# Sums of yb on chip, x added in the output stage, and second products accumulated onto a bank that ScalarE filled

## The chip, the cores and the metric

The kernel runs on one core of a Trainium2 chip. TensorE (PE) multiplies into PSUM banks, VectorE (DVE), ScalarE (ACT) and GpSimd (POOL) work on elements, and SyncE (SP) mostly issues DMA transfers. POOL issues those that add to their destination; ACT can issue transfers too. The metric is the device time of one execution in microseconds (us); less is better.

## The reference

One decoder layer in float32 on 512 tokens of 1024 features. All matrix products of this text come from it:

```python
h = x @ w_in[i]
ua, va, za, qh, kh, vh, zb, ga, gb = jnp.split(h, IN_OFFSETS, axis=-1)
...
ya = ua * sa.reshape(bn, s_len, A_WIDTH) * jax.nn.silu(za)
...
yb = o.reshape(bn, s_len, B_WIDTH) * jax.nn.silu(zb)

merged = jax.nn.sigmoid(ga) * (ya @ w_branch_a[i]) + jax.nn.sigmoid(gb) * (yb @ w_branch_b[i])
mix_out = merged @ w_out[i]

ple = jax.nn.sigmoid(x @ w_ple_gate[i]) * (p[i] @ w_ple[i])

x = layer_norm(DEEPNORM_ALPHA * x + mix_out + ple, ln_g[i], ln_b[i])
```

`sa` is a gated product within chunks of the normalised gelu of `va`; `o` is differential attention with eight heads, RMS-normalised.

## The kernel before

**Precision.** Each operand is cut into a high part (rounded, type fp32r) and a low part (what is left); a product of two operands is three matmuls, high by high, high by low and low by high. ScalarE writes the high part of a weight (line 407) and VectorE the low part (line 410); 128x1024 elements at a time are one unit of 512 KB. `cut_part` does the same for an activation (ScalarE's high, then VectorE's low four matmuls later, line 1276).

**Quads.** Eight products of 512x1024 by 1024x1024 (named v, va, zq, ga, gb, pg, wb, wa) are made by Strassen's scheme in Winograd's form (seven products of quarters in place of eight). `quad` runs seven steps. A step is two halves (t = 0 and 1) of 12 matmuls, each half into a PSUM bank of its own, so a quad is 168 matmuls. Three pairs of banks are used: Y by steps 1 and 5 to 7, X by step 2, Z by steps 3 and 4. Step 1 makes the first product P1 in Y, step 2 makes P2 in X, and the sum P1 + P2 is the first quarter of the result. Before: ScalarE copies Y to SBUF behind step 1 (`keep`, line 658), and behind step 2 VectorE adds X to it (`block`, line 663). Y goes on accumulating from step 5.

The left operands of steps 1 and 2 and of the last are quarters themselves; those of steps 3 to 6 are sums and differences of quarters, called s1, n4, s2 and s3. For the quads on x they lie in two tiles `xsh` and `xsl` (high and low, four slots each); the same tiles, called `ys`, later hold the sums of yb, then those of ya.

**Weights.** The right operands are sums of quarters of the weight, too. Some are made ahead in DRAM. The others are made in place in a ring of eight buffers: once a unit has been cut, `follow` has POOL issue a DMA that adds the next quarter to the same buffer (line 382), so a chain of up to four units goes through one buffer, each link used two steps after the one before. wa has no sums made ahead and eight such transfers; gb and pg have six.

**Order.** Every engine takes its instructions in program order. The program is written along the matmuls: `later(n, fn)` runs `fn` when n more matmuls have been written. So a number in the tables at the head (YB11, GATES, RESIDUE, ...) says behind which matmul of its quad an operation stands in its engine's queue; it starts when it is at the head of that queue and its operands are there.

**Stages.** Attention with its projections, then ua and part of za, then the quads va, zq, ga, gb, pg, the small product ple (48 matmuls), the quads wb (yb) and wa (ya), and the output product: a first half of 96 matmuls, a second of 120. What the change touches:

- the sums of yb (`sums_of`): eight pieces. VectorE adds (line 728), ScalarE cuts (line 735), VectorE takes the low part (line 739), and ScalarE issues two stores of 256 KB a piece to DRAM (line 731), four pieces in the stage of ua and four in gb. In pg SP issues eight loads of 512 KB back into `ys` (line 1136).
- the sums of ya: POOL adds in place (line 1288) in pg and wb, then `cut_part`.
- `residue` (line 1330): for each of four row blocks POOL issues a DMA that adds 512 KB of x to `base`, from wb's 180th matmul on and 36 apart, which is in wa. `base` holds the embedding term; `residual` (line 1408) adds the output product to it.
- `mb_done` (line 1352) multiplies wb's blocks by their gate on VectorE. `merge` (lines 1385 and 1387) multiplies wa's blocks by their gate, adds wb's (POOL for the upper half of the tokens), and a number of matmuls later (`MERGE`) PE transposes the result (line 1393) through two banks, from which ScalarE (line 1396) and VectorE (line 1397) make the operands of the output product.

Of the kernel before, what the change touches and what calls it, by code (L numbers as in the profile page):

```python
# [70 lines left out]
SUMS_OF_Y = (84, 139, 162, 180, 43, 82, 113, 157)  # L71
# [4 lines left out]

HELD = 2
# [3 lines left out]
YA22, YA_S1, YA_S3, YA_CUT_S1 = (4, 35), (24, 60), (40, 76), (90, 97)  # L81
YB11, YB12, YB22, LOAD_YS = (28, 43), (52, 59), (170, 177), (76, 100, 124, 148)
# [5 lines left out]
MERGE = (24, 15)  # L88
RESIDUE = (180, 36)
# [154 lines left out]
def hybrid_layer(ctx: ExitStack, tc: tile.TileContext, a, out: bass.AP):  # L244
# [397 lines left out]
    def operands(h, l, parts, last=4):  # L642

        s1, s2, n4, s3 = parts if callable(parts[0]) else [of_sum(parts, c) for c in range(4)]
        return (of_parts(h, l, 0, 0), of_parts(h, l, 4, 0), s1, n4, s2, s3, of_parts(h, l, last, 2 * P))

    def quad(name, left, banks, place, done):
# [8 lines left out]
        def keep(key, bank):  # L656
            kept[key] = tmp[0](key[0])[:, :bank.shape[-1]]
            act.activation(kept[key], bank, AF.Copy)  # L658
# [33 lines left out]
        steps = ((Y, True, after1), (X, True, after2), (Z, True, after5), (Z, False, None),  # L692
# [19 lines left out]

    ysd = dram.tile([2, 8, P, T], F32, name="ysd")

    def sums_of(source, store_to, tile_of, kp, at, steps):
        made = {}

        def quarter(k, t):
            return source[:, k:k + 2, t * 2 * P:(t + 1) * 2 * P]

        def piece(j):
            x11, x12 = quarter(2 * kp, 0), quarter(4 + 2 * kp, 0)
            x21, x22 = quarter(2 * kp, 1), quarter(4 + 2 * kp, 1)
            op, x, y = ((OP.subtract, x21, x22), (OP.subtract, made.get(0), x11),
                        (OP.add, made.get(1), x12), (OP.subtract, x11, x21))[j]
            m, h, l = tile_of(j)
            made[j] = m
            dve.tensor_tensor(out=m, in0=x, in1=y, op=op)

            def store(i, part):  # L730
                act.dma_start(out=store_to[i, 2 * j + kp],
                              in_=part.rearrange("p a b -> p (a b)").bitcast(F32))

            def high():
                act.activation(h, m, AF.Copy)
                store(0, h)

            def low():
                dve.tensor_tensor(out=l, in0=m, in1=h.bitcast(F32), op=OP.subtract)
                later(5, store, 1, l)  # L740

            later(steps[0], high)
            later(steps[1], low)

        for i, n in enumerate(at):
            later(n, piece, i)
# [300 lines left out]
    y_made = []  # L1047

    def of_stacks(j):
        hl = ap_.tile([P, 2, 2, 2 * P], F32R, name="yhl", tag="k", bufs=3)  # L1050
        if j % 2 == 0:
            y_made.append(ap_.tile([P, 2, 2, 2 * P], F32, name="ym", tag="q", bufs=3))
        return y_made[-1][:, j % 2], hl[:, 0], hl[:, 1]

    sums_of(yb[0], ysd, of_stacks, 0, SUMS_OF_Y[:4], (10, 18))


# [75 lines left out]

    def load_sum(parts, source, c):
        for i, part in enumerate(parts):
            sp.dma_start(out=part[:, c].rearrange("p (e a) t -> p e (a t)", e=2).bitcast(F32),
                         in_=source[i, 2 * c:2 * c + 2].rearrange("e p t -> p e t"))
# [106 lines left out]
    y_tiles = []  # L1244

    def of_norm(j):
        if not y_tiles:
            y_tiles.extend(late.tile([P, 2, 2, 2 * P], F32 if n == "g" else F32R, name="ys" + n, tag=n) for n in "gb")
        return y_tiles[0][:, j % 2], y_tiles[1][:, 0], y_tiles[1][:, 1]

    sums_of(yb[0], ysd, of_norm, 1, SUMS_OF_Y[4:], (10, 18))
    quad("gb", of_x, pairs(True), lambda c, t: None, gate_done("gb"))
    phl = []

    def load_p():
        phl.append(late.tile([P, 2, 2, T], F32R, name="phl", tag="R"))
        for k in range(2):
            pt = tmp[0]("pt")
            sp.dma_start(out=pt, in_=a["pT"][k * P:(k + 1) * P, :])
            later(40 + 12 * k, cut, phl[0][:, 0, k, :], phl[0][:, 1, k, :], pt)  # L1260

    later(64, load_p)
    base = post.tile([P, NT, D], F32, name="base", tag="V")

    def embedding_gate(c, t, z, source):
        act.activation(z, source, AF.Sigmoid)
# [19 lines left out]
    def add_ya(to, op, x, y, part):  # L1286
        (z,), (x,), (y,) = (part_of((ua,), *q, part) for q in (to, x, y))
        pool.tensor_tensor(out=z, in0=x, in1=y, op=op)  # L1288

    def slot(c):  # L1290
        return lambda part: (tile[:, c, 2 * part:2 * part + 2, :] for tile in ys)
# [15 lines left out]
    in_parts(cut_ya, YA22, 1, 1, (0, 1))  # L1307
# [6 lines left out]
    for n, c in zip(LOAD_YS, (0, 2, 1, 3)):  # L1314
        later(n, load_sum, ys, ysd, c)
# [35 lines left out]
    def mb_done(c, t, z, source):  # L1351
        dve.tensor_tensor(out=z, in0=source, in1=gate.pop(("gb", c, t)), op=OP.mult)
# [18 lines left out]
    for t in range(NT):  # L1371
        later(RESIDUE[0] + RESIDUE[1] * t, residue, t)
    quad("wb", operands(xh, xl, ys), pairs(True), place_b, mb_done)
# [10 lines left out]
    def merge(c, t, z, source):  # L1384
        dve.tensor_tensor(out=z, in0=source, in1=gate.pop(("ga", c, t)), op=OP.mult)
        early = t < NT // 2
        (pool if early else dve).tensor_tensor(out=z, in0=z, in1=mb[0][:, t, c * T:(c + 1) * T], op=OP.add)
        later(MERGE[not early], merge_turn, c, t, z)

# [11 lines left out]
    quad("wa", operands(xh, xl, of_ya, 0), pairs(False), lambda c, t: None, merge)  # L1401
# [20 lines left out]

    units = []
# [80 lines left out]
```

## Time and profile before

| what | value |
|---|---|
| median of 3 runs | 630.97 us (630.57 to 633.01) |
| the profiled execution | 631.1 us, span 629.1 us |
| PE busy | 610.4 us, 97% of the span |
| DVE, ACT, POOL busy | 474.4, 337.9, 139.7 us |
| moved by DMA | 146.91 MB, 234 GB/s over the span |

The span goes from the first to the last instruction of the program; the execution's own time is longer. A matmul's end is modelled and matmuls overlap, so how fast PE runs is read from the starts of matmuls or from how many fall into a window. Names such as `wr<-in_w` are tiles: what is written, then what is read; `wh` and `wl` are a weight's high and low part, `xsh` and `xsl` the slots of sums, `ps_...` PSUM banks. A wait is put down to what ended last before it.

### The profile page before, as it was taken

To read this page: it belongs to the slowest core of one execution; us is meant where nothing else is said; L and a number is where in the kernel's file an instruction comes from. 1 tells how busy PE (TensorE), PEld (TensorE's weight loads), DVE (VectorE), ACT (ScalarE), POOL (GpSimd) and SP (SyncE) were. 2 spreads that over 40 slices of the span, in tenths; PEclk is the share of its full clock that TensorE was granted. 3 is DMA by queue.
4 is the path that set the end of the run, shared out by engine and by line. 5 is a ranking of instruction groups with operands and counts; after the bars stand their busy time and mean duration, and the time that the engine had idled before them with its cause. 6 is when DMAs were issued, how large, how long until landed. Compare 5 with 4: busy or idle time off the path is not lost.

```text
span 629.1 us, 8655 instructions
## 1 busy us (share of the span) xinstructions
PE 610.4 (97%) x3012; PEld 511.4 (81%) x3012; DVE 474.4 (75%) x800; ACT 337.9 (54%) x540; POOL 139.7 (22%) x144
## 2 busy tenths in 40 slices
PE   9999999999999999999999999999999999977995
PEld 6888888888888888888899888888778778766884
DVE  6996687788788767768578877678967796749376
ACT  6555654744745755489565655556653563424100
POOL 1234030341440530230111211113400322520012
PEclk9999999999999999999999999999999999988999
DMA  8689899587888796888988898899798489994002
GB/s 302 215 245 186 268 282 289 210 219 248 287 235 274 217 319 207 230 222 320 258 284 237 210 244 241 238 260 299 190 328 333 160 224 237 262 259 167 1 33 101
DMA packets 50111, 146.91 MB, mean 234 GB/s; under 512 B 6420, under 2 KB 7572, under 8 KB 49748
## 3 DMA queue, kind: packets, MB, share of 16 engines
q1 hardware_dynamic: 37268, 106.91, 47.9%
q0 software_dynamic: 9920, 34.87, 30.1%
q10 hardware_dynamic: 2880, 4.59, 2.0%
q8 instruction: 24, 0.39, 0.3%
q14 instruction: 19, 0.16, 0.1%
HBM read 123.14 MB, written 34.73 MB: 251 GB/s over the span
## 4 chain that ended last, share of the span: by engine, by line
PE 82%; DMA 7%; issue 5%; DVE 3%; ACT 1%; POOL 1%; DVEq 0%; POOLq 0%; ACTq 0%
PE ps_pp L278 51%; PE ps_sc L278 12%; DMA wr<-in_w 7%; PE ps_tx L278 7%; PE ps_sc L826 3%; PE ps_po L871 3%; PE ps_tr L860 1%; PE ps_po L278 1%; PE ps_tr L278 1%; DVE wl L410 1%; DVE xl L1276 1%; ACT wh L407 1%; POOL ua L1288 1%; PE ps_po L482 1%; PE ps_tr L1213 1%
## 5 line engine op out<-in xcount | busy, mean ns | idle before, releaser
L410 DVE TENSOR_TENSOR wl<-wr,wh 128x1024 fp32r<-128x1024 f32 (+1 forms) x143 | 178.7, 1254 | 46.9 <-ACT wh L407 46.4
L407 ACT ACTIVATE wh<-wr 128x1024 fp32r<-128x1024 f32 (+1 forms) x143 | 147.0, 1033 | 86.3 <-PE ps_sc L278 28.0
L278 PE MATMUL ps_pp<-xh,wh 128*128 128x512 f32 (+1 forms) x276 | 109.5, 397 | 0.0
L278 PE MATMUL ps_pp<-xl,wh 128*128 128x512 f32 (+1 forms) x276 | 107.0, 388 | 0.0
L278 PE MATMUL ps_pp<-xh,wl 128*128 128x512 f32 (+1 forms) x276 | 105.4, 382 | 0.0
L278 PE MATMUL ps_pp<-wl,xh 128*128 128x512 f32 (+1 forms) x168 | 64.6, 385 | 0.0
L278 PE MATMUL ps_pp<-wh,xh 128*128 128x512 f32 (+1 forms) x168 | 64.5, 384 | 0.0
L278 PE MATMUL ps_pp<-wh,xl 128*128 128x512 f32 (+1 forms) x168 | 64.5, 384 | 0.0
L839 ACT ACTIVATE p<-p,sth 128x128 f32<-128x128 f32 (+3 forms) x64 | 35.5, 555 | 47.4 <-DVE sth L837 47.3
L278 PEld LDWEIGHTS ps_pp<-xh,wl 128*128 128x128 f32 x276 | 52.1, 189 | 8.7
L278 PEld LDWEIGHTS ps_pp<-xh,wh 128*128 128x128 f32 x276 | 52.1, 189 | 8.6 <-ACT wh L304 0.7
L278 PEld LDWEIGHTS ps_pp<-xl,wh 128*128 128x128 f32 x276 | 52.1, 189 | 8.2 <-DVE xl L305 0.4
L382 POOL DMA_DIRECT2D wr<-in_w x34 | 29.8, 875 | 126.4 <-DVE wl L410 113.8
L771 POOL TENSOR_TENSOR hl<-m,hl 128x512 fp32r<-128x512 f32 x16 | 25.1, 1608 | 54.7 <-ACT hl L766 54.7
L278 PEld LDWEIGHTS ps_pp<-wl,xh 128*128 128x128 f32 x168 | 32.0, 190 | 6.2 <-DVE wl L410 0.3
L278 PEld LDWEIGHTS ps_pp<-wh,xl 128*128 128x128 f32 x168 | 32.0, 191 | 6.0
L278 PEld LDWEIGHTS ps_pp<-wh,xh 128*128 128x128 f32 x168 | 31.9, 190 | 6.1
L278 PE MATMUL ps_pp<-wh,xsh 128*128 128x512 f32 x80 | 32.2, 402 | 4.6 <-ACT s L658 4.6
L278 PE MATMUL ps_sc<-wl,xsh 128*128 128x512 f32 x88 | 34.5, 392 | 1.2 <-DVE wl L410 1.1
L833 DVE CUSTOM_DVE_ANT_0 p<-ps_sc,mask 128x128 f32<-128x128 f32 (+3 forms) x64 | 30.9, 483 | 5.6 <-PE ps_sc L826 5.6
L278 PE MATMUL ps_sc<-wh,xsh 128*128 128x512 f32 x88 | 34.5, 392 | 0.2 <-ACT s L658 0.2
L278 PE MATMUL ps_sc<-wh,xsl 128*128 128x512 f32 x88 | 34.3, 390 | 0.0
(312 smaller groups left out, 1267.3 us busy)
## 6 DMA issues: line engine op xcount, KB each, us to landing
wr<-in_w SPq DMA_DIRECT2D x81, 512.0 KB, 5.1
wr<-in_w POOLq DMA_DIRECT2D x30, 512.0 KB, 6.9
k<-hl SPq DMA_DIRECT2D x16, 256.0 KB, 5.4
q<-hl SPq DMA_DIRECT2D x16, 256.0 KB, 4.2
ws_va<-in_w POOLq DMA_DIRECT2D x8, 512.0 KB, 10.5
wr<-ws_va SPq DMA_DIRECT2D x8, 512.0 KB, 4.2
wa<-in_w POOLq DMA_DIRECT2D x6, 512.0 KB, 7.4
kx<-hl SPq DMA_DIRECT2D x12, 256.0 KB, 5.4
```

The costliest lines, as they stand in the source:

```text
L278: pe.matmul(ps, s, m, start=start, stop=stop, skip_group_check=read_within)
L382: pool.dma_start(out=raw[u][:, :n], in_=weights(STEPS[FOLLOWS[u]][1], n), accum_op=OP.add)
L407: act.activation(h, raw[u][:, :width(STEPS[u][0])], AF.Copy)
L410: dve.tensor_tensor(out=l, in0=raw[u][:, :width(STEPS[u][0])], in1=h.bitcast(F32), op=OP.subtract)
L482: pe.matmul(idle, zeros[:, :P], zeros, start=True, stop=True)
L771: pool.tensor_tensor(out=hl[:, 3 - j, :], in0=m[2 * j], in1=hl[:, j, :].bitcast(F32), op=OP.subtract)
L826: pe.matmul(sc[m][:, :n], q[:, m, i * P:(i + 1) * P], kk[:, m, :n], start=o == 0, stop=o == 1)
L833: dve.tensor_tensor_reduce(out=pr[m][:, :n], in0=sc[m][:, :n], in1=mask[:, T - n:], scale=-(DK ** -0.5), scalar=3e38, op0=OP.add, op1=OP.m ...
L839: act.activation(pr[m][:, :n], pr[m][:, :n], AF.Exp, bias=st[:, m:m + 1], scale=-1.0, accum_out=st[:, 2 + m:3 + m])
L860: pe.transpose(tr[:, j * P:(j + 1) * P], ad[:, j * P:(j + 1) * P], ident)
L871: pe.matmul(po[:, i * P:(i + 1) * P], at[:, j * P:(j + 1) * P], v[:, j, h * P:(h + 1) * P], start=j == 0, stop=j == i)
L1213: pe.matmul(sa[:, t * P:(t + 1) * P], va[:, t, g * P:(g + 1) * P], aux[0][:, 0, g, :], start=True, stop=True)
```

## The change

Three edits, with the numbers of the tables set anew.

1. The sums of yb are no longer made in `sums_of`, stored and loaded. POOL makes them in place in yb (`add_yb`, four adds in gb, four in pg), and `cut_part` cuts them straight into the slots of `ys` in pg, each behind the step that last reads the slot. The quarter 22 of yb is cut in gb into the quarter 21 of `xh` and `xl`, that of ya in ple into the quarter 22; wb and wa read them there. The sums of ya move from pg and wb to ple and wb.
2. In v, gb, pg, wb and wa (`GOES_ON`) ScalarE copies P1 from bank Y into bank X, and step 2 accumulates P2 onto it. VectorE's add of the first quarter falls away. What follows it (a sigmoid, a multiplication by the gate, in v a copy) reads bank X.
3. The four transfers of x are issued in the first half of the output stage, behind matmuls 2, 8, 26 and 32.

Beside these, POOL takes four multiplications from VectorE (two in `mb_done`, two in `merge`), and the later transposes of the merges stand 22 or 23 matmuls behind their merge, not 15.

```diff
+GOES_ON = ('v', 'gb', 'pg', 'wb', 'wa')
...
-MERGE = (24, 15)
-RESIDUE = (180, 36)
+MERGE = {'early': 24, 1: 23, 0: 22}
+RESIDUE = (2, 8, 26, 32)
...
+        goes_on = name in GOES_ON
+
         def after1(t):
-            keep(("s1", t), Y[t])
+            if goes_on:
+                act.activation(X[t], Y[t], AF.Copy)
+            else:
+                keep(("s1", t), Y[t])
 
         def after2(t):
+            if goes_on:
+                z = place(0, t)
+                return done(0, t, tmp[0]("s1")[:, :X[t].shape[-1]] if z is None else z, X[t])
             s1 = kept.pop(("s1", t))
             block(0, t, X[t], s1, OP.add, s1)
...
-        steps = ((Y, True, after1), (X, True, after2), (Z, True, after5), (Z, False, None),
+        steps = ((Y, True, after1), (X, not goes_on, after2), (Z, True, after5), (Z, False, None),
...
-    sums_of(yb[0], ysd, of_stacks, 0, SUMS_OF_Y[:4], (10, 18))
...
-    sums_of(yb[0], ysd, of_norm, 1, SUMS_OF_Y[4:], (10, 18))
...
+    def add(tile, to, op, x, y, part):
+        (z,), (x,), (y,) = (part_of((tile,), *q, part) for q in (to, x, y))
+        pool.tensor_tensor(out=z, in0=x, in1=y, op=op)
...
+    in_parts(cut_yb, YB22, 1, 1, (0, 1))
+    in_parts(add_yb, YB_S1, (1, 1), OP.subtract, (0, 1), (1, 1))
+    in_parts(add_yb, YB_S3, (0, 1), OP.subtract, (0, 0), (0, 1))
     quad("gb", of_x, pairs(True), lambda c, t: None, gate_done("gb"))
...
     in_parts(cut_yb, YB11, 0, 0, (0, 0))
     in_parts(cut_yb, YB12, 1, 0, (1, 0))
-    in_parts(cut_yb, YB22, 1, 1, (1, 1))
+    in_parts(add_yb, YB_S2, (0, 0), OP.subtract, (1, 1), (0, 0))
+    in_parts(add_yb, YB_N4, (1, 0), OP.add, (0, 0), (1, 0))
+    in_parts(cut_yb, YB_CUT_S1, 1, 1, slot(0))
+    in_parts(cut_yb, YB_CUT_N4, 1, 0, slot(2))
+    in_parts(cut_yb, YB_CUT_S2, 0, 0, slot(1))
+    in_parts(cut_yb, YB_CUT_S3, 0, 1, slot(3))
+    in_parts(cut_ya, YA22, 1, 1, (1, 1))
     in_parts(add_ya, YA_S1, (1, 1), OP.subtract, (0, 1), (1, 1))
     in_parts(add_ya, YA_S3, (0, 1), OP.subtract, (0, 0), (0, 1))
     in_parts(cut_ya, YA_CUT_S1, 1, 1, first_sum)
-    for n, c in zip(LOAD_YS, (0, 2, 1, 3)):
-        later(n, load_sum, ys, ysd, c)
...
     def mb_done(c, t, z, source):
-        dve.tensor_tensor(out=z, in0=source, in1=gate.pop(("gb", c, t)), op=OP.mult)
+        by = pool if c == 1 and t < 2 else dve
+        by.tensor_tensor(out=z, in0=source, in1=gate.pop(("gb", c, t)), op=OP.mult)
...
-    for t in range(NT):
-        later(RESIDUE[0] + RESIDUE[1] * t, residue, t)
...
     def merge(c, t, z, source):
-        dve.tensor_tensor(out=z, in0=source, in1=gate.pop(("ga", c, t)), op=OP.mult)
         early = t < NT // 2
+        by = pool if early and c else dve
+        by.tensor_tensor(out=z, in0=source, in1=gate.pop(("ga", c, t)), op=OP.mult)
         (pool if early else dve).tensor_tensor(out=z, in0=z, in1=mb[0][:, t, c * T:(c + 1) * T], op=OP.add)
-        later(MERGE[not early], merge_turn, c, t, z)
+        later(MERGE["early" if early else c], merge_turn, c, t, z)
...
+    for t, n in enumerate(RESIDUE):
+        later(n, residue, t)
```

POOL's queue in wa up to the output stage, before (`wr_...` are accumulating weights, `base<-in_x` is a transfer of x, the `s_...` rows are merges):

```order
L382 DMA wr_4858<-in_w 128x1024
L1330 DMA base<-in_x 128x1024
L382 DMA wr_4829<-in_w 128x1024
L382 DMA wr_4858<-in_w 128x1024
L1387 TENSOR_TENSOR s_5090<-s_5090,mb 128x512
L1330 DMA base<-in_x 128x1024
L1387 TENSOR_TENSOR s_5110<-s_5110,mb 128x512
L382 DMA wr_4961<-in_w 128x1024
L382 DMA wr_4991<-in_w 128x1024
```

and now, a few rows further on:

```order
L384 DMA wr_4785<-in_w 128x1024
L384 DMA wr_4813<-in_w 128x1024
L1349 TENSOR_TENSOR s_5212<-s_5212,gates 128x512
L1350 TENSOR_TENSOR s_5212<-s_5212,mb 128x512
L1349 TENSOR_TENSOR s_5234<-s_5234,gates 128x512
L1350 TENSOR_TENSOR s_5234<-s_5234,mb 128x512
L1293 DMA base<-in_x 128x1024 x4
```

The transfers of x stood between the accumulating weights; they now stand behind the last of them and behind the last merges on POOL.

SP's queue in pg, before (`xsh<-ysd` and `xsl<-ysd` load the sums of yb):

```order
L1136 DMA xsl<-ysd 128x2x512
L367 DMA wr_4546<-in_w 128x1024
L367 DMA wr_4561<-in_w 128x1024
L1136 DMA xsh<-ysd 128x2x512
L1136 DMA xsl<-ysd 128x2x512
L367 DMA wr_4596<-in_w 128x1024
L367 DMA wr_4612<-ws_wb 128x1024
```

and now:

```order
L1258 DMA pt<-in_pT 128x512 x2
L369 DMA wr_4488<-in_w 128x1024
L369 DMA wr_4505<-in_w 128x1024
L369 DMA wr_4540<-in_w 128x1024
L369 DMA wr_4558<-ws_wb 128x1024
```

Nothing stands between the weights any more.

VectorE's queue in wb where the first quarter is finished, before (`wl` is a weight's low part, `xl<-ua` the low part of a quarter of ya):

```order
L1276 TENSOR_TENSOR xl<-ua,xh 128x2x256
L663 TENSOR_TENSOR mb<-ps_pp,s_4777 128x512
L1352 TENSOR_TENSOR mb<-mb,gates 128x512
L410 TENSOR_TENSOR wl<-wr_4639,wh 128x1024
L663 TENSOR_TENSOR mb<-ps_pp,s_4799 128x512
L1352 TENSOR_TENSOR mb<-mb,gates 128x512
```

and now:

```order
L1211 TENSOR_TENSOR xl<-ua,xh 128x2x256
L1316 TENSOR_TENSOR mb<-ps_pp,gates 128x512
L412 TENSOR_TENSOR wl<-wr_4584,wh 128x1024
L1316 TENSOR_TENSOR mb<-ps_pp,gates 128x512
L1211 TENSOR_TENSOR xl<-ua,xh 128x2x256
L412 TENSOR_TENSOR wl<-wr_4597,wh 128x1024
```

Each multiplication by the gate reads the PSUM bank, and the add ahead of it is gone.

More of the change, by code (lines that the diff above doesn't have):

```diff
@@ L709, in quad @@
                     later(1, after, t)
[L713 to L746, printed above, removed]
     stacks = {}
@@ L1132, in hybrid_layer @@
     of_x = operands(xh, xl, xs)
[L1134 to L1137, printed above, removed]
     def cut_x(kp, c):
@@ L1243, in hybrid_layer @@
     quad("ga", of_x, pairs(False), lambda c, t: None, gate_done("ga"))
[L1244 to L1249, printed above, removed]
-    sums_of(yb[0], ysd, of_norm, 1, SUMS_OF_Y[4:], (10, 18))
[L1252 to L1266, printed above, removed]
     ys = xs
@@ L1284, in cut_ya, with add_ya, add_yb @@
         cut_part(source, where, part)
-    def add_ya(to, op, x, y, part):
-        (z,), (x,), (y,) = (part_of((ua,), *q, part) for q in (to, x, y))
+    def add(tile, to, op, x, y, part):
+        (z,), (x,), (y,) = (part_of((tile,), *q, part) for q in (to, x, y))
         pool.tensor_tensor(out=z, in0=x, in1=y, op=op)
+    def add_ya(*what):
+        add(ua, *what)
+    def add_yb(*what):
+        add(yb[0], *what)
     def slot(c):
@@ L1370, in hybrid_layer @@
     in_parts(cut_ya, YA_CUT_S2, 0, 0, slot(1))
-    for t in range(NT):
-        later(RESIDUE[0] + RESIDUE[1] * t, residue, t)
-    quad("wb", operands(xh, xl, ys), pairs(True), place_b, mb_done)
+    quad("wb", operands(xh, xl, ys, 0), pairs(True), place_b, mb_done)
     norm_last = []
@@ L1400, in hybrid_layer @@
     of_ya = [of_first_sum, of_sum(ys, 1), of_sum(ys, 2), of_sum(ys, 0)]
-    quad("wa", operands(xh, xl, of_ya, 0), pairs(False), lambda c, t: None, merge)
+    quad("wa", operands(xh, xl, of_ya), pairs(False), lambda c, t: None, merge)
     zst = [small([P, 2 if t < NT - 1 else 3, 6], "vst", 4) for t in range(NT)]
```

26 lines of the change are left out of this document (16 added, 10 removed).

## The prediction

> **What bounds the kernel now.** I read the page's first two parts, then the chain of waits, then sums by window, then the DMA answers. The page:
>
> ```profile
> span 629.1 us, 8655 instructions
> ...
> PE 610.4 (97%) x3012; PEld 511.4 (81%) x3012; DVE 474.4 (75%) x800; ACT 337.9 (54%) x540; POOL 139.7 (22%) x144
> ...
> PEclk9999999999999999999999999999999999988999
> DMA  8689899587888796888988898899798489994002
> ```
>
> TensorE bounds it, but a busy PE is modelled, so the question is how far each stage is from TensorE's own pace. The profiled execution took 631.1 us, its span 629.1, so 2.0 us lie around the span; the median of the runs shown is 630.97, 0.1 below. The granted clock dips at one place, slices 36 and 37, where the one stretch ends in which the DMA engines are at 9 three times running (34 to 36). The chain of waits from 281 us on and from 431 us on gives the pace (first and last row) and what stands between matmuls:
>
> ```profile
> 292.13 10.88 PE ps_sc L278 x48
> ...
> 452.85 10.22 DMA wr<-in_w
> ...
> 496.68 1.22 DVE wl L410
> ...
> 524.21 10.41 DMA wr<-in_w
> ...
> 537.32 7.88 DMA wr<-in_w
> ...
> 547.89 17.83 DMA wr<-in_w
> ...
> 575.10 0.44 PE ps_tr L1393 x4
> ```
>
> 48 matmuls take 10.88 us, 0.2267 each, so the 168 of a quad take 38.1. The sums by window, cut at the first matmul of gb, pg, wb, wa and of the output stage's first half (columns: length, busy time and count of each engine, granted clock, DMA share, GB/s):
>
> ```profile
> 388.42:431.94 43.52, 43.52 (x218) 36.90 (x217) 32.64 (x39) 24.20 (x32) 5.19 (x6) 1.00 0.94 255
> 431.94:473.07 41.13, 39.58 (x178) 32.27 (x176) 31.95 (x35) 27.59 (x39) 10.89 (x8) 1.00 0.93 273
> 484.23:524.36 40.13, 38.92 (x170) 31.25 (x169) 33.42 (x36) 22.75 (x30) 9.66 (x8) 1.00 0.69 208
> 524.36:576.76 52.40, 45.15 (x193) 35.95 (x192) 32.61 (x37) 20.42 (x26) 15.24 (x15) 0.93 0.99 252
> 576.76:599.48 22.72, 22.72 (x105) 18.80 (x104) 12.12 (x16) 5.69 (x7) 0.00 (x0) 1.00 0.00 1
> ```
>
> The counts beyond 168 (less one or two that straddle an edge) are transposes: six sets of eight in gb, one in pg, none in wb, six sets of four in wa. A set of four costs 0.44 (last row of the chain), one of eight twice that. What is above pace is then: gb 43.5 - 38.1 - 5.3 = 0.1; pg 41.1 - 38.1 - 0.9 = 2.1; wb 40.1 - 38.1 = 2.0; wa 52.4 - 38.1 - 2.6 = 11.7. Together 15.9 us, three quarters in wa. The timeline of wa shows how they arise:
>
> ```profile
> 551.80 1.06 ACT L407 ACTIVATE wh<-wr 128x1024 fp32r<-128x1024 f32 x1 [5.46 <-DMA wr<-in_w]
> ...
> 557.08 0.50 PE L278 MATMUL ps_pp<-wh,xsh 128*128 128x512 f32 x1 [3.21 <-ACT s L658]
> ...
> 558.01 0.63 PE L278 MATMUL ps_pp<-wh,xsh 128*128 128x512 f32 x1
> 558.43 0.63 PE L278 MATMUL ps_pp<-wl,xsh 128*128 128x512 f32 x1
> ...
> 570.10 0.66 PE L1393 MATMUL ps_po<-ident,s 128*128 128x128 f32 x4 [3.42 <-DVE xl L1397]
> ```
>
> ScalarE's cut waits 5.46 us for a weight, TensorE then waits 3.21, and for some eight matmuls afterwards the steps are 0.42 us instead of 0.2267 (558.01 to 558.43): a stall of over 3 us costs about 1.7 more at half clock. The second stall names a VectorE instruction, but the chain follows it to the accumulating weight that took 17.83 us. DMA in wa's window, and two rows of the page:
>
> ```profile
> q0 software_dynamic: 1728, 6.29, 60.9%
> q1 hardware_dynamic: 2438, 6.89, 37.5%
> ...
> wr<-in_w POOLq DMA_DIRECT2D x7, 512.0 KB, 10.4
> ...
> base<-in_x POOLq DMA_DIRECT2D x4, 512.0 KB, 11.1
> ```
>
> ```profile
> q1 hardware_dynamic: 37268, 106.91, 47.9%
> ...
> wr<-in_w POOLq DMA_DIRECT2D x30, 512.0 KB, 6.9
> ```
>
> All accumulating transfers go through q0: here eight weights and the four of x, 1728 / 12 = 144 packets each. 60.9% of 52.4 us is 31.9 us of all engines, 2.66 us a transfer. So wa is DMA-bound for its length (share 0.99), and an accumulating weight takes 10.4 us there, against a median of 6.9 over the run.
>
> **The change, part by part.**
>
> *x to the output stage.* wa loses 4 x 2.66 = 10.6 us of DMA time: 0.99 x 52.4 = 51.9 falls to 41.3, against TensorE's 38.1 + 2.6 = 40.7. What an accumulating weight may take follows from the code: its chain is used every second step, 48 matmuls, 10.9 us; ScalarE's cut (1.06, above), VectorE's (1.22, chain) and POOL's issue (0.88, below) leave 7.7. At 6.9 nothing stalls; at 10.4 each of three links is 2.7 late, 8.1 us. So 3.6 to 11.7 us come back. I take 9.7: the load becomes gb's (0.94 of a stage with 0.1 above pace), not today's, and some two us stay since the gate and weight loads still bunch. In the output stage's first half the DMA engines are idle (share 0.00), and that is the cover. The first residual follows 50 matmuls in, at 11.3 us, the third 98 in, at 22.2. The first transfer is asked for 2 matmuls in: it lands at 0.5 + 6.9 = 7.4 us. The last, 32 in, lands behind three others by 7.3 + 10.6 = 17.9. Cost 0; at today's 11.1 the first is 0.3 late, and what queues behind it on VectorE is cuts for the second half, 21.8 us in.
>
> *yb's sums on chip.* Sixteen stores and eight loads through DRAM go. By the page's q1 row 47.9% of 629.1 is 301 us for 106.91 MB, 1.48 us per 512 KB: 11.8 us of loads leave pg and ple, where they stood in SP's queue between weights, and as much of stores gb and the stage of ua. The weight of the chain's row at 452.85 took 10.22 us; at 6.9 it is 3.3 earlier, and pg's stall hangs on it. I count 1.8 of 2.1 back (bounds 0 and 2.1). The adds move to POOL:
>
> ```profile
> L1288 POOL TENSOR_TENSOR ua<-ua 128x512 f32<-128x512 f32 x8 | 14.5, 1817 | 48.1 <-DVE xl L1276 43.9 <-DMA wr<-in_w 4.2
> 491.97 2.21 DVE L410 TENSOR_TENSOR wl<-wr,wh 128x1024 fp32r<-128x1024 f32 x1 [0.26 <-ACT wh L407]
> 494.09 0.68 DVE L1276 TENSOR_TENSOR xl<-ua,xh 128x512 fp32r<-128x512 f32 x1
> 494.70 0.68 DVE L663 TENSOR_TENSOR mb<-ps_pp,s 128x512 f32<-128x512 f32 x1
> ```
>
> An add takes POOL 1.82 us. gb gets four where it had none (POOL busy 5.2 of 43.5 us); in pg four on yb take the place of four on ya, and those go to ple and wb. Beside such an add VectorE's cut takes 2.21 instead of 1.22 us (second row). VectorE keeps eight low cuts of yb's sums and loses eight adds of 0.68. Counted by the program's order, gb loses nine operations of 0.68 and gets two, some 5 us less; pg gets eight cuts and loses seven other operations, so it stays near 32.6 of 41 us. ScalarE's eight cuts, 0.6 each, all move to pg, which loses four: 30 of 41. Cost 0, bound 1.
>
> The Trainium skill (GPSIMD Engine Reference, Specifications) speaks against this edit: GpSimd shares its SBUF interfaces with VectorE and contends with VectorE instructions that have two SBUF inputs, as the cuts have. The trace agrees, by the 2.21. What that rule alone would make of the time is rival B.
>
> *The second product on a filled bank.* Ten copies, two in each of five quads, now end on TensorE's path:
>
> ```profile
> 527.27 0.60 ACT L658 ACTIVATE s<-ps_pp 128x512 f32<-128x512 f32 x1 [1.66 <-PE ps_pp L278]
> 530.44 1.06 ACT L407 ACTIVATE wh<-wr 128x1024 fp32r<-128x1024 f32 x1 [2.57 <-DMA wr<-in_w]
> 531.41 0.58 ACT L658 ACTIVATE s<-ps_pp 128x512 f32<-128x512 f32 x1
> 524.21 0.88 POOL L382 DMA_DIRECT2D wr<-in_w  x1 [0.26 <-DVE wl L410]
> ```
>
> The copy takes 0.60 us and waits for nothing but TensorE. 12 matmuls of the other half, 2.72 us, lie between a bank's end and its accumulation, so 2.1 us are spare: cost 0. Into PSUM the copy is not in the trace; between 0.58 and twice that it stays covered. Cover goes only where a late weight stands ahead of it on ScalarE, as at 530.44. Each quad loses two VectorE adds of 0.68. In wb the cut at 496.68, for which TensorE waits, stands behind an add of a first product: it starts 0.7 earlier, and the next behind both. I count 1.3 of wb's 2.0 back (bounds 0.3 and 2.0).
>
> *Merges.* POOL takes four more multiplications, two of them ahead of TensorE's transposes. Like its adds they take 1.28 or 2.21 us:
>
> ```profile
> 538.43 1.28 POOL L1387 TENSOR_TENSOR s<-s,mb 128x512 f32<-128x512 f32 x1 [0.24 <-DVE s L1385]
> ...
> 540.35 2.21 POOL L1387 TENSOR_TENSOR s<-s,mb 128x512 f32<-128x512 f32 x1
> ```
>
> Two of 1.28 fit into the 24 matmuls (5.4 us) between the merge and its transposes; two of 2.21 leave 1.0 us, and the other half queues behind. Up to 1.2 us, taken as part of wa's two.
>
> The sum: 631.1 - 9.7 - 1.8 - 1.3 = 618.3, 618 as the median.
>
> **The rivals.**
>
> *A: the accumulating weights stay late in wa.* They hang on each other and still meet gates, norm rows and output weights. For it: the 41.3 us of DMA demand is still TensorE's 40.7. Against: about 10 of it serve the output stage and may be late. At 10.4 us as now, 3.6 return in wa and with pg's and wb's the time is 631.1 - 6.7 = 624.4.
>
> *B: no gain, by POOL's contention.* Twelve POOL operations more (eight adds, four multiplications) at 1.0 us of VectorE time each are 12; if all fell on TensorE's path, 618.3 + 12 = 630. Against: VectorE is idle for 7 to 20 us in each of these windows, and the same windows lose adds.
>
> *C: slower, by POOL's queue.* In gb and pg the yb adds stand among the accumulating weights in POOL's order, and each add waits for a low cut on VectorE. The later weight of gb's third pair shows what is spare:
>
> ```profile
> 411.38 0.86 POOL L382 DMA_DIRECT2D wr<-in_w  x1 [0.87 <-DMA ysd<-ysb]
> ```
>
> Landed 6.9 us later (418.3) and cut (2.3), it is ready at 420.6 for the last step, which begins at 388.4 + 144 x 0.2267 + 5 x 0.88 = 425.5: 4.9 us. From there a delay stalls TensorE as in wa, 3.2 + 1.7. Two weights in two quads are 4 x 4.9 = 20: 618 + 20 = 638. It decides when POOL's adds hold a weight back by 5 us. Against: the adds of gb and pg are due before, or with, the third pair's cuts, so one add of 1.8 to 2.2 us is the most.
>
> **How the numbers follow.** The forecast (615 to 622) has 0.70, A (622 to 627.8) 0.18, B 0.06, C 0.06. Under 615.2 all 15.9 us would have to come back. The range, 614.5 to 626.5, leaves out B, C and A's end. A measurement here tells 0.5%, 3.2 us, from no change: faster is the forecast and A, 0.88; same is B, 0.06; slower is C, 0.06.
>
> **What would show it.** In the profile after: wa near 43 us with a DMA share below 0.99 and accumulating weights at 7 to 8 us; no TensorE wait of 3 us, and a clock of 1.00 there; pg near 39.3, wb near 39; four x transfers in the output stage's first half, landed before any residual waits; TensorE waiting for no copy into PSUM. I am wrong if accumulating weights in wa still take 10 us, if TensorE waits for POOL at a transpose, or if the output stage grows past 45 us.

## The result, and the profile after

The changed kernel takes 622.88 us (median of 4 runs, 622.02 to 623.50) against 630.89 for the kernel before (630.57 to 633.01): a ratio of 0.9866, with a 95% interval of 0.9847 to 0.9885. It is 8.0 us faster; 12.8 had been forecast, with a range of 614.5 to 626.5. The profiled executions differ by 631.1 - 622.6 = 8.5 us, their spans by 8.2.

The first parts of the page of the changed kernel:

```profile
span 620.8 us, 8616 instructions
...
PE 607.7 (98%) x3012; PEld 508.5 (82%) x3012; DVE 470.4 (76%) x778; ACT 338.3 (54%) x542; POOL 156.6 (25%) x156
...
PEclk9999999999999999999999999999999999999998
```

The dip of the clock in slices 36 and 37 is gone. The busy shares tell little, as before. The sums by window do, cut at the same places (gb, pg, wb, wa, the output stage's first half; the columns are those of the prediction):

```profile
388.39:432.09 43.70, 43.70 (x218) 36.74 (x216) 31.41 (x32) 23.15 (x30) 10.01 (x10) 1.00 0.79 212
432.09:471.65 39.56, 39.52 (x178) 32.27 (x176) 33.82 (x35) 28.46 (x42) 9.79 (x9) 1.00 0.84 220
482.80:522.38 39.58, 38.87 (x169) 31.30 (x168) 32.74 (x35) 22.74 (x30) 13.55 (x10) 1.00 0.67 212
522.38:566.31 43.93, 41.80 (x190) 33.04 (x188) 30.26 (x30) 20.18 (x25) 18.88 (x17) 1.00 0.96 245
566.31:591.24 24.93, 23.42 (x109) 19.11 (x108) 14.85 (x19) 5.93 (x7) 0.00 (x0) 1.00 0.44 98
```

| stage | before | after | returned | forecast |
|---|---|---|---|---|
| gb | 43.52 | 43.70 | -0.2 | 0 |
| pg | 41.13 | 39.56 | 1.6 | 1.8 |
| wb | 40.13 | 39.58 | 0.5 | 1.3 |
| wa | 52.40 | 43.93 | 8.5 | 9.7 |
| output, first half | 22.72 | 24.93 | -2.2 | 0 |

The rows sum to 8.2, the difference of the spans. One set of four transposes (0.44 us) now falls behind the edge between the last two rows, as the count of matmuls shows (105 before, 109 after). Without that shift wa returned 8.0 and the output stage cost 1.8.

The last row is the surprise. POOL's and SP's queues around the edge (the timeline; start, length, and for an instruction that waited the idle time and what ended it), then the merge on VectorE and the transpose on TensorE, and the row of the chain of waits on the same load:

```profile
558.35 2.13 POOL L1350 TENSOR_TENSOR s<-s,mb 128x512 f32<-128x512 f32 x1
560.42 3.55 POOL L1293 DMA_DIRECT2D base<-in_x  x4
...
559.80 0.39 SPq L1323 DMA_DIRECT2D gates<-gate_ga  x1
...
568.87 0.69 DVE L1349 TENSOR_TENSOR z<-ps_pp,gates 128x512 f32<-128x512 f32 x1 [1.60 <-DMA gates<-gate_ga]
...
570.94 0.66 PE L1356 MATMUL ps_po<-ident,z 128*128 128x128 f32 x4 [1.51 <-DVE xl L1360]
...
559.80 8.95 DMA gates<-gate_ga
```

The prediction had the first transfer of x asked for two matmuls into the output stage, some 0.5 us behind 566.3. It was asked for at 560.4, six microseconds ahead of that stage, and the other three directly behind it. Nothing that these transfers read or write was outstanding, so POOL issued them as soon as its last merge was done. They then ran beside the last load of a gate, asked for at 559.80. It took 8.95 us, and VectorE's merge and TensorE's transpose waited for it.

### The profile page after: what moved, and what is told of

Read it like the earlier page. It is cut to its first block, busy times and chain, and to the rows that moved or that the text cites. A ratio compares the mean times of both kernels' runs of the same rounds, so it can differ in the third digit from the quotient of the medians.

```text
span 620.8 us, 8616 instructions
## 1 busy us (share of the span) xinstructions
PE 607.7 (98%) x3012; PEld 508.5 (82%) x3012; DVE 470.4 (76%) x778; ACT 338.3 (54%) x542; POOL 156.6 (25%) x156
## 4 chain that ended last, share of the span: by engine, by line
PE 85%; DMA 6%; DVE 4%; issue 3%; ACT 1%; POOL 1%; DVEq 0%; SPq 0%; POOLq 0%; ACTq 0%
PE ps_pp L280 52%; PE ps_sc L280 15%; PE ps_tx L280 6%; PE ps_sc L801 3%; DMA wr<-in_w 3%; PE ps_po L846 3%; DMA gates<-gate_ga 1%; DVE wl L412 1%; PE ps_tr L835 1%; PE ps_po L280 1%; PE ps_tr L280 1%; DMA wr<-ws_wb 1%; DVE base L1290 1%; PE ps_tr L1172 1%; PE ps_po L1172 1%
## 5 line engine op out<-in xcount | busy, mean ns | idle before, releaser
L412 DVE TENSOR_TENSOR wl<-wr,wh 128x1024 fp32r<-128x1024 f32 (+1 forms) x143 | 190.2, 1334 | 45.6 <-ACT wh L409 43.4
```

Source lines behind the costliest of these rows:

```text
L412: dve.tensor_tensor(out=l, in0=raw[u][:, :width(STEPS[u][0])], in1=h.bitcast(F32), op=OP.subtract)
```

## The experiments

In the names, a_ stands for the changed kernel with one thing altered, b_ for the kernel before, h_ for a_x_held. Of the h_ runs, h_s2_dve starts from h_best. Each run is compared with the kernel before on its own chip, so ratios are what is compared (0.001 is 0.63 us); lengths of stages come from one profiled execution each.

| run | median us | ratio (95% interval) | wa | output, first half |
|---|---|---|---|---|
| the change | 622.88 | 0.9866 (0.9847 to 0.9885) | 43.93 | 24.93 |
| a_no_x | 621.27 | 0.9833 (0.9818 to 0.9847) | 44.72 | 23.22 |
| a_x_held | 620.87 | 0.9829 (0.9812 to 0.9846) | 44.68 | 23.20 |
| a_x_back | 626.24 | 0.9918 (0.9901 to 0.9935) | 49.42 | 23.24 |
| b_x_moved | 634.60 | 1.0042 (1.0027 to 1.0057) | 45.61 | 32.41 |
| b_x_held | 624.18 | 0.9893 (0.9874 to 0.9911) | 45.61 | 23.30 |
| h_no_seed | 622.75 | 0.9860 (0.9843 to 0.9877) | 44.57 | |
| h_yb_dram | 622.75 | 0.9860 (0.9843 to 0.9876) | | |
| h_mult_dve | 620.62 | 0.9826 (0.9810 to 0.9843) | 43.96 | 23.23 |
| h_mult_late | 623.65 | 0.9875 (0.9859 to 0.9892) | 42.72 | 27.12 |
| h_best | 619.24 | 0.9814 (0.9799 to 0.9828) | 42.93 | 23.20 |
| h_no_s2 | 619.75 (one run) | | | |
| h_s2_dve | 618.90 | 0.9808 (0.9792 to 0.9823) | 43.80 | |

### x in the output stage

Five runs ask what the x transfers cost and where. The first two start from the changed kernel: without them, and with POOL held ahead of them.

```diff
     def merge(c, t, z, source):
...
+        if (c, t) == (0, 2):
+            pool.tensor_tensor(out=small([P, 1], "held", 1), in0=z[:, :1], in1=z[:, :1], op=OP.add)
```

> The changed kernel without the four transfers of x (x is not added to the output). Theory T: the 2.2 us by which the output stage's first half grew (22.7 to 24.9) are the x transfers' doing: POOL reached them at 560.4 us, six microseconds before that half begins, and they ran beside the last load of a gate (559.8 to 568.7 us, 8.95 us), which a merge and with it a transpose on TensorE waits for. Then the last gate takes 4.5 to 6 us here, the half lasts 22.7 to 23.2, wa stays at 43.9, and the time falls by about 2 us, to some 621. Rival S: the gate is late because it stands behind weights in SP's queue and its buffer comes free late, whatever x does: then the half stays at 24.5 to 25 and the time within 0.5 us of the changed kernel's 622.9. Rival W: the x transfers are what keeps wa's weights slow: then wa falls as well, below 42.5.

> The changed kernel, with POOL held ahead of the x transfers by one addition on one column that reads the first merge of the output stage (the one that needs the last gate). T: the transfers start after that merge, some 566 to 568 us, so the last gate takes 4.5 to 6 us, TensorE does not wait 1.5 us for its transpose, the half lasts 22.7 to 23.2, the four transfers land by 580, and the time is 620.5 to 621.3 against the changed kernel's 622.9 (ratio to the kernel before about 0.984). S: the half stays at 24.5 to 25 and the time at 622.9. A third way: the transfers, now later, land after the residuals ask for them (579 us), which delays VectorE and with it the second half: then the half is short and the end is not, 622 or more.

Held, the timeline of POOL and of VectorE, and the windows of wa and of the output stage's first half:

```profile
569.20 0.19 POOL L1352 TENSOR_TENSOR held<-z 128x1 f32<-128x1 f32 x1 [8.19 <-DVE z L1350]
569.42 3.56 POOL L1293 DMA_DIRECT2D base<-in_x  x4
...
578.67 0.69 DVE L1373 SCALAR_TENSOR_TENSOR base<-ps_pp,base 128x512 f32<-128x512 f32 x1 [3.56 <-PE ps_pp L280]
```

```profile
522.15:566.83 44.68, 42.05 (x189) 33.07 (x188) 30.32 (x30) 20.20 (x25) 15.39 (x13) 1.00 0.93 237
566.83:590.03 23.20, 23.20 (x109) 19.13 (x108) 14.76 (x19) 5.93 (x7) 3.76 (x5) 1.00 0.56 114
```

POOL now idles 8.2 us for the merge and issues the transfers at 569.4, inside the stage. The stage takes 23.20, with TensorE busy throughout, and the first residual waits for TensorE alone, so the transfers are hidden as the prediction meant. A kernel without any x gets the same length, 23.22. Both times, 621.3 and 620.9, are where T had them. S falls, since the gate came in time once x was elsewhere (6.3 and 5.9 us from issue to landing), and W falls, since wa did not shrink without x. It was even 0.8 longer than T had it: in both runs TensorE waits there, 0.8 and 0.6 us, for a copy of ScalarE's (line 660) behind a late weight, which the change's profile doesn't show. Why that weight came later is open.

The other three runs are the kernel before with x alone moved, and then held too, and the changed kernel with x back in wa.

```diff
-RESIDUE = (2, 8, 26, 32)
+RESIDUE = (180, 36)
...
+    for t in range(NT):
+        later(RESIDUE[0] + RESIDUE[1] * t, residue, t)
     quad("wb", operands(xh, xl, ys, 0), pairs(True), place_b, mb_done)
```

> The changed kernel with the x transfers back at the 180th matmul from wb's begin on, 36 apart. If the move of x carries the gain in wa, wa goes back to 48 to 52 us, its accumulating weights to about 10 us, the output stage's first half to 22.7, and the time is 626 to 630. If the other edits carry it, wa stays under 46 and the time is at most 624.

> The kernel before with the x transfers alone moved to where the change has them. The prediction gave 9.7 us of wa's 11.7 to this move. If it carries that, wa falls from 52.4 to 43 to 46 us, and with the output stage's first half longer by about 2 (T) the time is 623 to 627. If the other edits carried part of it (the seeded accumulation takes two additions off VectorE per quad, and wb's and wa's transfers start at another phase), wa stays at 47 to 52 and the time at 627 to 631.

> The kernel before with the x transfers alone moved, and held on POOL by one addition on one column behind the first merge of the output stage. With the move alone and not held, the output stage's first half grew from 22.7 to 32.4 us, since the last gate, asked at 563.5 behind the x transfers of 562.0 to 563.6, took 13.98 us and TensorE waited 7.3 for its merge. T: held, the half is 22.7 to 23.5, wa stays near 45.6, and the time is 624 to 626. Rival: without the other edits the merges of the output stage are late for another reason (transposes 15 matmuls behind their merge, not 22): the half stays over 25 and the time over 627.

Moved alone, x made the kernel slower. Wa fell from 52.40 to 45.61, as the first of its two expectations had it, but the output stage's first half took 32.41, and the time missed both. Its chain of waits, TensorE's timeline and the two queues:

```profile
563.50 13.98 DMA gates<-gate_ga
...
579.16 1.08 PE L1391 MATMUL ps_po<-ident,z 128*128 128x128 f32 x4 [7.33 <-DVE z L1385]
...
561.95 3.58 POOL L1330 DMA_DIRECT2D base<-in_x  x4
...
563.50 0.52 SPq L1359 DMA_DIRECT2D gates<-gate_ga  x1
...
570.74:603.15 32.41, 25.08 (x105) 20.42 (x104) 13.39 (x17) 5.69 (x7) 0.00 (x0) 0.89 0.28 68
```

Here the gate was asked for 1.6 us behind the first transfer of x and took 13.98 us; in the change it was asked for 0.6 us ahead of it and took 8.95. TensorE waited 7.3, and the granted clock of the stage fell to 0.89. Nothing in the program ties the two queues together, so which comes first follows from what each queue has waited for until then. With the transfers held, the same kernel has the stage at 23.30 and the whole at 0.9893: the one added column was worth 1.5% there (1.0042 to 0.9893), and 0.4% on the change.

With x back in wa, the changed kernel has wa at 49.42 (the time, 626.2, is at the low end of what the first expectation gave), and by the median its accumulating weights are hardly slower than without any x. The DMA views of wa's window, first with x back, then without x:

```profile
wr<-in_w POOLq DMA_DIRECT2D x7, 512.0 KB, 10.6
wr<-in_w SPq DMA_DIRECT2D x7, 512.0 KB, 7.3
...
gates<-gate_ga SPq DMA_DIRECT2D x3, 512.0 KB, 13.1
```

```profile
q0 software_dynamic: 1152, 4.19, 49.2%
...
wr<-in_w POOLq DMA_DIRECT2D x7, 512.0 KB, 10.0
wr<-in_w SPq DMA_DIRECT2D x7, 512.0 KB, 5.2
gates<-gate_ga SPq DMA_DIRECT2D x3, 512.0 KB, 6.3
```

The median of the accumulating weights goes from 10.6 to 10.0 only. What x lengthens is the last of them, and the transfers of SP. With x back the chain of waits goes through the last one:

```profile
546.27 17.30 DMA wr<-in_w
```

Without x the chain goes through the second of the last four; the other row is the DMA view of the moment (544.31) at which the last is asked for:

```profile
540.51 9.99 DMA wr<-in_w
...
wr<-in_w POOLq DMA_DIRECT2D x1, 512.0 KB, 11.7
```

POOL's timeline without x shows why 10 us and more remain: the last four are asked for within five microseconds.

```profile
539.37 0.88 POOL L384 DMA_DIRECT2D wr<-in_w  x1 [1.39 <-DVE wl L412]
540.51 0.86 POOL L384 DMA_DIRECT2D wr<-in_w  x1 [0.26 <-DVE wl L412]
542.24 0.87 POOL L384 DMA_DIRECT2D wr<-in_w  x1 [0.86 <-DVE wl L412]
544.31 0.86 POOL L384 DMA_DIRECT2D wr<-in_w  x1 [1.20 <-DVE wl L412]
```

By the queue's row a transfer takes 49.2% of 44.72 us over 8 = 2.75 us of all engines, so four of them fill 11 us whoever else is there. They land in the order in which they were asked for: at 548.2, 550.5, 553.0 and 556.0 without x; with x back at 550.2, 553.7, 556.1 and 563.6, with a transfer of x at 559.8 between the last two. Each transfer of x in that row puts one such time more in front of what follows.

### The filled bank, and the sums of yb

Both start from a_x_held, and each puts one edit back as it was before.

```diff
-GOES_ON = ('v', 'gb', 'pg', 'wb', 'wa')
+GOES_ON = ()
```

> The kernel with the held x transfers (620.9 us, 0.983 of the kernel before) with GOES_ON empty: ScalarE copies P1 to SBUF and VectorE adds P2 again, as before. The prediction gave the filled bank 1.3 us in wb and nothing elsewhere. Then wb goes from 39.6 back to 40.2 to 40.9, gb, pg and wa stay within 0.4, and the time is 621.5 to 622.5. If VectorE's additions were hidden anyway, nothing moves: 620.9 within 0.6. If the filled bank costs TensorE something (gb got 0.2 longer with the change), gb falls back to 43.5 and the time to 620.5 or less.

```diff
-    in_parts(add_yb, YB_S1, (1, 1), OP.subtract, (0, 1), (1, 1))
...
+    sums_of(yb[0], ysd, of_stacks, 0, SUMS_OF_Y[:4], (10, 18))
...
+    for n, c in zip(LOAD_YS, (0, 2, 1, 3)):
+        later(n, load_sum, ys, ysd, c)
```

> The kernel with the held x transfers with the sums of yb made and stored as before (VectorE's additions, 16 stores, 8 loads; the additions of ya in pg and wb as before), the other edits kept. The prediction gave this edit 1.8 us in pg. Then pg goes from 39.3 back to 40.9 to 41.2, wb and wa stay, and the time is 622.3 to 623.2. If the contention of POOL and VectorE eats a part of the edit's gain, or wb pays for it, wb falls below 39.2 here and the time is under 622.

The windows of wb without the filled bank and of pg with the sums through DRAM; with the edits these are 39.57 and 39.32:

```profile
482.05:522.62 40.57, 39.19 (x170) 31.22 (x169) 34.63 (x37) 22.75 (x30) 13.53 (x10) 1.00 0.65 204
```

```profile
431.64:471.95 40.31, 39.28 (x177) 32.35 (x176) 31.45 (x33) 27.97 (x39) 9.87 (x8) 1.00 0.93 273
```

The filled bank is worth 1.0 us in wb, between the prediction's bounds of 0.3 and 2.0 and near its 1.3. Yb's sums are worth 1.0 in pg in these executions, 1.6 between the two kernels; over all the profiles pg took 40.3 to 41.1 with the sums through DRAM (four kernels) and 39.1 to 39.6 with them on chip. gb took 43.7 in every kernel with the sums on chip and 43.52 in each of the four with them through DRAM, so the 0.2 that gb lost is that edit's. By the ratios each edit is worth 0.3%, about as much as the intervals leave open.

### POOL's operations

In the changed kernel TensorE's two longest waits in wa name POOL:

```profile
537.29 0.66 PE L1356 MATMUL ps_po<-ident,s 128*128 128x128 f32 x4 [0.81 <-POOL s L1350]
...
560.53 0.66 PE L1356 MATMUL ps_tr<-ident,s 128*128 128x128 f32 x4 [1.03 <-POOL s L1350]
...
553.37 1.29 POOL L1349 TENSOR_TENSOR s<-s,gates 128x512 f32<-128x512 f32 x1 [7.71 <-DVE s L665]
554.74 1.29 POOL L1350 TENSOR_TENSOR s<-s,mb 128x512 f32<-128x512 f32 x1
555.99 2.28 POOL L1349 TENSOR_TENSOR s<-s,gates 128x512 f32<-128x512 f32 x1
```

Three runs on a_x_held put operations back on VectorE: the two multiplications of `merge`; these, with the early transposes later; and all four multiplications, with only the first pair's transposes later.

```diff
-        by = pool if early and c else dve
+        by = dve
```

> The kernel with the held x transfers with the two multiplications of merge back on VectorE. Theory P: POOL's four operations on the second pair of merges (1.29, 1.29, 2.28, 2.13 us, 553.4 to 560.5 in the changed kernel) are more than the 24 matmuls (5.4 us) that lie ahead of the transposes, and cost TensorE the wait of 1.0 us at 559 us with what follows it. Then that wait goes, wa falls from 44.7 to 43.2 to 43.8 and the time to 619.4 to 620.1. Rival V: the two multiplications, 0.7 us each, then stand ahead of weight cuts on VectorE, and TensorE waits for those: wa stays within 0.4 of 44.7, the time at 620.5 to 621.3.

```diff
-MERGE = {'early': 24, 1: 23, 0: 22}
+MERGE = {'early': 30, 1: 23, 0: 22}
```

> As the one with the multiplications of merge on VectorE, and the early merges' transposes 30 matmuls behind their merge, not 24. P: the first wait for POOL too (0.8 us at 536 us; its merge starts late since VectorE's cut of a late weight stands ahead of it) is then covered by 1.4 us more, and wa falls to 42.3 to 43.0, the time to 618.5 to 619.4. Rival: the wait is the late weight's, and only changes its name; wa stays where the multiplications alone leave it.

```diff
-        by = pool if c == 1 and t < 2 else dve
-        by.tensor_tensor(out=z, in0=source, in1=gate.pop(("gb", c, t)), op=OP.mult)
+        dve.tensor_tensor(out=z, in0=source, in1=gate.pop(("gb", c, t)), op=OP.mult)
...
-MERGE = {'early': 24, 1: 23, 0: 22}
+MERGE = {'early': (30, 24), 1: 23, 0: 22}
```

> The kernel with the held x transfers, all four multiplications that the change gave to POOL back on VectorE, and the transposes of the first two early merges 30 matmuls behind their merge, those of the second two 24. With the multiplications of merge on VectorE alone wa was 43.97 and the time 620.6 (0.983); the later transposes of all four took both waits for POOL away, but put VectorE's low cut of one transpose behind two merges and cost 2.2 us in the output stage. P: here the first wait goes and the output stage stays at 23.2: wa 43.0 to 43.4; in wb the wait at 516 us (0.1, with its slow step 0.27) goes; the time is 619.0 to 620.0. Rival: VectorE's four more operations of 0.69 make weight cuts late: wb or wa longer than 39.6 and 44.0, the time 620.5 to 622.

With the multiplications on VectorE the second wait went and wa fell by 0.7, less than the 0.9 to 1.5 that P gave, since a wait for VectorE (0.85 at 561 us) grew in its place; the time moved by less than its interval. With all early transposes later wa fell to 42.72, but the output stage lost 3.9 us. VectorE's timeline and TensorE's wait show how:

```profile
566.75 0.69 DVE L1350 TENSOR_TENSOR z<-z,mb 128x512 f32<-128x512 f32 x1
567.37 0.68 DVE L1362 TENSOR_TENSOR xl<-ps_tr,xh 128x512 fp32r<-128x512 f32 x1
...
568.20 0.63 PE L1358 MATMUL ps_tr<-ident,s 128*128 128x128 f32 x4 [2.15 <-DVE xl L1362]
```

The low cut that frees the bank `ps_tr` now stands behind a merge of the output stage on VectorE, and the next transpose into that bank waits for it. The wait is 2.15 us, but TensorE's next matmuls start 0.43 us apart, not 0.2267, and the granted clock of that stage is 0.94; with some nine matmuls at that pace this makes up the rest of the 3.9. The rival of that run had the wait only changing its name inside wa; it moved to the next stage instead. With only the first pair later, both waits for POOL are gone, wa is 42.93, wb 39.23 and the output stage 23.20: 0.9814, faster than the change by half a per cent. Holding x gives 0.4% of that (0.9829); the rest, 0.15%, is inside the intervals.

In wb another wait was left, 0.6 us for a weight's low cut. Two runs ask whether POOL's additions beside it are its cause.

```diff
-    in_parts(add_ya, YA_S2, (0, 0), OP.subtract, (1, 1), (0, 0))
```

> The kernel with the held x transfers without the two additions on POOL that make the sum s2 of ya in wb (the slot then holds a plain quarter, so the output is that of another s2). In wb TensorE waits 0.6 us at 495 for a weight's low cut that takes VectorE 2.00 us beside the second of these additions, where one alone takes 1.22. If the contention is the cause, the cut takes 1.2, the wait goes, and wb falls from 39.6 to 38.7 to 39.0. If the cut is late for what stands ahead of it (a quarter of ya and a gate multiplication, 0.68 each), wb stays at 39.4 to 39.6.

```diff
-YA11, YA12, YA_S2, YA_N4 = (26, 33), (50, 57), (44, 52), (68, 76)
+YA11, YA12, YA_S2, YA_N4 = (26, 33), (50, 57), (59, 66), (70, 78)
...
-    in_parts(add_ya, YA_S2, (0, 0), OP.subtract, (1, 1), (0, 0))
+    in_parts(add_ya_dve, YA_S2, (0, 0), OP.subtract, (1, 1), (0, 0))
```

> The kernel with the x transfers held and the four multiplications on VectorE (619.2 us, 0.981), with the two additions that make s2 of ya in wb on VectorE too, 15 matmuls later, so behind the weight cut that was slow beside them on POOL. If contention alone makes that cut late (without these additions wb was 38.67), the cut at 493 takes 1.2 us, TensorE's wait at 494 goes, and wb falls from 39.23 to 38.5 to 38.8; the time is 618.3 to 619.0, less than the comparison can tell. Rival: VectorE's two additions of 0.69 make the next cuts or the second sum n4 late, and wb is 39.2 or more.

The rows of a_x_held (VectorE, POOL, TensorE), then VectorE's cuts with the additions on VectorE and later, and that kernel's window of wb:

```profile
490.37 2.27 DVE L412 TENSOR_TENSOR wl<-wr,wh 128x1024 fp32r<-128x1024 f32 x1 [0.26 <-ACT wh L409]
...
493.76 2.00 DVE L412 TENSOR_TENSOR wl<-wr,wh 128x1024 fp32r<-128x1024 f32 x1
...
493.38 1.30 POOL L1223 TENSOR_TENSOR ua<-ua 128x512 f32<-128x512 f32 x1 [1.83 <-DVE xl L1211]
...
495.82 0.50 PE L280 MATMUL ps_sc<-wl,xsh 128*128 128x512 f32 x1 [0.61 <-DVE wl L412]
```

```profile
490.08 1.22 DVE L412 TENSOR_TENSOR wl<-wr,wh 128x1024 fp32r<-128x1024 f32 x1 [0.26 <-DMA wr<-ws_wb]
...
492.43 1.22 DVE L412 TENSOR_TENSOR wl<-wr,wh 128x1024 fp32r<-128x1024 f32 x1
...
482.29:520.58 38.29, 38.29 (x169) 31.42 (x168) 31.74 (x39) 22.74 (x30) 7.38 (x6) 1.00 0.69 218
```

Without the additions wb took 38.67 (and the whole 619.75, in one execution); with them on VectorE 38.29, which is TensorE's pace, and the wait is gone in both. In both runs both cuts take some 1.22 us again, so the wait was contention, and two VectorE operations of 0.69 behind the cut cost less than two of POOL's at 1.30 beside it. POOL's additions at that later place were not tried. In a_x_held the second cut ends 1.08 us after POOL's addition (494.68 to 495.76), and so does the first (491.56 to 492.64; its addition starts at 490.26): each cut needs nearly its whole 1.22 us once POOL is done. The Trainium skill (GPSIMD Engine Reference, Specifications) says that POOL contends with VectorE instructions that have two SBUF inputs; these rows agree, with 0.8 to 1.05 us for a cut. The whole time, 0.9808 (0.9792 to 0.9823), can't be told from the kernel without this edit. Its wa was 43.80, longer by 0.9: an accumulating weight came late in wa's second step, and ScalarE's copy into the bank stood behind its cut, as the prediction had said it could:

```profile
528.36 1.06 ACT L409 ACTIVATE wh<-wr 128x1024 fp32r<-128x1024 f32 x1 [4.27 <-DMA wr<-in_w]
529.32 0.58 ACT L672 ACTIVATE ps_tx<-ps_pp 128x512 f32<-128x512 f32 x1
...
529.96 0.50 PE L280 MATMUL ps_tx<-wh,xh 128*128 128x512 f32 x1 [1.05 <-ACT ps_tx L672]
```

So of wb's 0.9 nothing is left at the end of wa. Whether that weight was late by chance, or because wb became shorter while the transfers kept their pace, is open.

## Why the prediction was right, and where it was not

The time, 622.9, is inside the range, but in the band that the prediction gave rival A (622 to 627.8, chance 0.18), not in the forecast's own (615 to 622, 0.70). All three signs that it named for being wrong came: accumulating weights near 10 us in wa (9.3), TensorE waiting for POOL at a transpose (0.81 and 1.03), an output stage above 45 us (47.2).

**What bounds the kernel** held: the gain came out of the waits counted above the pace of 0.2267 us a matmul, some 8 of 10 us in wa, and no stage went below that pace.

**x out of wa.** The size was nearly right (8.0 returned, after the shift of a transpose, for 9.7), but x alone carries less of it: 5.5 us by putting it back into the changed kernel (4.7 against that kernel without any x), 6.8 by taking it out of the one before. Of the 3.0 us between 52.40 and 49.42, 0.4 are the shift and the rest belongs to the other edits; no run separates them. The mechanism was wrong in one number. The accumulating weights were to go from 10.4 to 7 or 8 us, as the load falls. They took 9.3 in the change and 10.0 without any x, because they are asked for in a bunch and go one behind the other. By the prediction's own rule (7.7 us a link, three links) 9.3 us would have returned 6.9, so that 9.7 came near 8.0 is in part luck. The gain came from the last of the bunch (17.83 before, 11.7 without x) and from SP's weights and gates. So the share of the DMA engines was not the right measure: it is 1.00 both in a_x_back (wa 49.42) and in b_x_moved (45.61). The number of transfers ahead on the accumulating queue fits all these runs, though none varies it alone.

**x into the output stage** is the step that failed. "The first transfer is asked for 2 matmuls in" took a place in the program for a time. The place says what stands ahead on POOL's queue, and nothing there waited for the output stage. So the cover, the idle DMA engines of that half, was missed by six microseconds, and cost 0 became 1.8. The whole output stage took 47.2 us, and 45.4 with the transfers held; before it took 45.0, which with the 0.4 of the shifted transposes is the same 45.4.

**Yb's sums on chip**: 1.6 of the 1.8 in pg; the contention put at 0 with a bound of 1 goes with the 0.2 lost in gb. VectorE did seven operations less there, as counted, but its busy time fell by 1.2 us and not by 5, since its fourteen weight cuts took 20.6 us in place of 17.1.

**The filled bank**: 1.3 forecast for wb, 0.5 returned. The bank alone gave 1.0. Two things stood against it. One is POOL's share of `mb_done`: with it back on VectorE wb fell by 0.35. The other is POOL's second addition: without the add of the first quarter the cut that TensorE waits for comes earlier, but now falls beside that addition, and takes 2.00 us in place of the 1.21 that it took before and in h_no_seed. The copies were covered in the change. In three of the later kernels a late weight uncovered one (0.4 to 1.05 us), on the condition that the prediction gave.

**Merges**: "up to 1.2 us" was taken as part of wa's two. TensorE waited 0.81 and 1.03 for POOL, 1.8 together, and wa kept 3.6 above pace.

**The rivals.** A had the weights' median nearly right, and the time fell into its band, but its sum (624.4) had 3.6 us back in wa where 8.0 came: the median was not what hurt. B's contention is real, and nearly of the size that B gave it (12 us of VectorE's time): the weight cuts took 11.5 us more over the run, by these rows of the two pages.

```profile
L410 DVE TENSOR_TENSOR wl<-wr,wh 128x1024 fp32r<-128x1024 f32 (+1 forms) x143 | 178.7, 1254 | 46.9 <-ACT wh L407 46.4
...
L412 DVE TENSOR_TENSOR wl<-wr,wh 128x1024 fp32r<-128x1024 f32 (+1 forms) x143 | 190.2, 1334 | 45.6 <-ACT wh L409 43.4
```

Little of that fell on TensorE's path, since VectorE has idle time: 0.2 in gb and 0.35 in wb, beside the waits for POOL in wa. 0.9 more in wb goes with additions of ya that stood there before too. C didn't happen: gb grew by 0.2 and pg got shorter. The sum was 4.6 too good by spans: 1.8 in the output stage, 1.7 in wa, 0.7 in wb, 0.4 in pg and gb.

## What to carry to other kernels

A transfer or an operation that is written later in the program isn't later in time unless something it needs is: look for what its queue waits for, and if there is nothing, make it depend on the event that it should follow; one column added on the issuing engine was enough here. When the cost of a transfer is counted, count what is asked for in the microseconds beside it: a load that stood next to four others took 9 to 14 us, not 5 to 7. And before an addition goes to POOL, look at what VectorE does in the same microsecond: if TensorE waits for that, an operation on VectorE behind it was cheaper here.

## What was not expected of the hardware

- Accumulating transfers on POOL's queue hold back a plain one on SP's queue, and a microsecond or two of order matters: the gate's 512 KB took 13.98 us when asked for 1.6 us behind the first of four, 8.95 when asked for 0.6 us ahead of it, and 7.04 in the kernel of the 13.98 with the four held.
- The median time of an accumulating transfer in wa was 10.4 to 10.6 us with four more of its kind in the stage; without them it was 9.8 and 10.0 in the changed kernel, 8.9 in the kernel before.
